# Value products of an attention kernel over 512 queries at a time, on one Trainium2 core

## The chip, the cores and the metric

The kernel runs on one core of one Trainium2 chip. Five engines work side by side and meet at semaphores: TensorE (matrix products; PE in the profile, its weight loads PEld), VectorE (DVE), ScalarE (ACT), GpSimd (POOL) and SyncE (SP), which here issues nearly all DMAs. The metric is the device time of one execution in microseconds; lower is better.

## The reference

One layer of an encoder: RMS norm, multi-head latent attention with a SiLU gate, output projection, residual, final RMS norm. Sequence 1024, width 1024, 8 heads, all float32. What matters here:

```
q  = rms_norm(c_q)  @ w_uq      # per head 128 "nope" + 64 rotary columns
kv = rms_norm(c_kv) @ w_ukv     # per head 128 key + 128 value columns
s  = q_nope @ k_nope.T + q_pe @ k_pe.T
p  = softmax(s * scale)         # 1024 x 1024 per head
o  = p @ v
y  = (o * silu(gate)) @ w_out + x
out = rms_norm(y)
```

## The kernel before

**Precision by splitting.** Each operand of a product is split into a high part, rounded to the matmul's input type, and a low part, the remainder. `mm3` (lines 58 to 61) makes a product from three matmuls: high by high, high by low, low by high. So the probabilities too must be split before they meet the values.

**Stages.** Up to about 193 us the kernel makes the latent projections, the rotary parts and the gate (`stream`, `rope_half`). From then to about 525 us it runs attention, and after that the output projection (`out_start`, `out_end`, `out_last`).

**Attention.** The work is cut into 64 units `u`, eight per head, each of 128 queries by 1024 keys. `scores(u)` makes ten matmuls of 512 columns into a PSUM tile `s`; VectorE takes the row maxima (`nmx`, line 462), ScalarE the exponentials with row sums (line 464), VectorE the reciprocal (line 469), GpSimd multiplies by it (line 470), and VectorE transposes 32 by 32 blocks in place (line 471). The result goes to one of two buffers `probs`.

Four units make a *group* of 512 queries; there are 16 groups. In a 32 by 32 transposed tile the keys lie on partitions inside each 32-row block only, so `exchange(g)` moves blocks between partitions by 16 DMAs of 128 KB on SP's queue, into tiles `d`. Before the change there are two tiles `d` per group, one for each pair of 32-query blocks `a` (index `two`), from a pool of two buffers of 8 KB per partition. So the tile of a half takes the room of the same half of the group before, and its DMAs wait until that half has been split.

`split_part(g, two)` splits one half's `d` into two pairs of tiles `pt_h`, `pt_l`, one for each half of the keys: ScalarE casts (line 489), VectorE subtracts (line 491, and half of the second at line 493), GpSimd subtracts the other half (line 494). There are three buffers of each. `values(g, two)` multiplies: 8 key tiles by 3 matmuls of 256 columns into half a PSUM bank `pv`, then two VectorE multiplications into `gate` (line 512).

**Order.** The loop over `u` issues `scores(u)`; `exchange(u // 4)` at every fourth unit; `split_part` at odd units from 7; `values` at even units from 8. The order on each engine isn't this one: a planner at build time sorts the instructions by priority and by when its own model says that their inputs are ready. `later(100)` puts `values` 100 steps back in priority, `later(150)` the loads of `qpe`. Production of q, k and v for the next heads (`produce_q`, `produce_k`, `produce_v`) and, at the last head, the loads of output weights (`load_w_out`, line 519) and of x (line 542) lie between. Each engine then runs its list strictly in the planned order.

**Memory.** SBUF is nearly full. Two unnamed tiles `pad_a` and `pad_b` only take up room.

Of the kernel before, what the change touches and what calls it, by code (L numbers as in the profile page):

```python
# [8 lines left out]
F32 = mybir.dt.float32  # L9
F32R = mybir.dt.float32r  # L10
# [4 lines left out]
P = 128  # L15
L = 1024
# [7 lines left out]
KD = D // P  # L24
HT = L // 2
# [4 lines left out]
def kernel(  # L30
# [21 lines left out]
    nc = tc.nc  # L52
    mm = nc.tensor.matmul

    def f32(ap):
        return ap.bitcast(F32)

    def mm3(ps, lh, ll, rh, rl, first, last):
        mm(ps, lhsT=lh, rhs=rh, start=first, stop=False)  # L59
        mm(ps, lhsT=lh, rhs=rl, start=False, stop=False)  # L60
        mm(ps, lhsT=ll, rhs=rh, start=False, stop=last)  # L61
# [5 lines left out]
    def later(steps):  # L67


        def wrap(fn):  # L70
            def run(*args):
                tc.cur_priority += steps
                result = fn(*args)
                tc.cur_priority -= steps
                return result

            return run

        return wrap

    const = ctx.enter_context(tc.tile_pool(name="const", bufs=1))
# [5 lines left out]


    g_sb = const.tile([P, KD + 5], F32, name="g_sb")
    const.tile([P, 72], F32, name="pad_a")  # L90
    qpe_d = dram.tile([H, 4, 32, L], F32, name="qpe_d")

    row_d = {name: dram.tile([P, KD], F32, name=f"{name}_d") for name in ("rx", "sq", "sk", "rq", "rk")}
    kk_h = const.tile([P, L], F32R, name="kk_h")
    kk_l = const.tile([P, L], F32R, name="kk_l")
    ss = const.tile([P, 2, KD], F32, name="ss")
    const.tile([P, 112], F32, name="pad_b")

    def acc(name):
        return ps_a.tile([P, 512], F32, name=name, tag="acc")  # L100

    def wide(name):
        return ps_s.tile([P, L], F32, name=name, tag="s")

    def halves(half):
        return slice(half * HT, (half + 1) * HT)
# [87 lines left out]
    gate = gpool.tile([P, H, L], F32, name="gate")  # L194
# [56 lines left out]
    def stream(m):  # L251
        wh, wl = [], []
        for kq in range(2):
            wh.append(gp.tile([P, 4, P], F32R, name=f"gwh_{m}_{kq}", tag="gwh"))
            wl.append(gp.tile([P, 4, P], F32R, name=f"gwl_{m}_{kq}", tag="gwl"))
            wr = gp.tile([P, 4, P], F32, name=f"gwr_{m}_{kq}", tag="gwr", bufs=2)
            nc.sync.dma_start(wr, wg[m - 3 - (m > 5), :, kq * 4:(kq + 1) * 4])
            split(wr, wh[-1], wl[-1])
        ps = wide(f"g_{m}")
        for k in range(KD):  # L260
            for half in range(2):
                hs = halves(half)
                mm3(ps[:, hs], wh[k // 4][:, k % 4], wl[k // 4][:, k % 4], xh[:, k, hs], xl[:, k, hs],
                    k == 0, k == KD - 1)
        return ps
# [8 lines left out]
    ps = stream(3)  # L274
    nc.scalar.copy(craw[3], ps)
    latent_sums((0, 1, 2), "sq")
    ps = stream(4)
# [11 lines left out]
    ps = wide("pe")  # L289
# [74 lines left out]
    for i in range(1, H):  # L364
# [7 lines left out]
        if i < 5:  # L372
            g, half = (i - 1) // 2, (i - 1) % 2
# [11 lines left out]
    at = ctx.enter_context(tc.tile_pool(name="attn", bufs=2, side="right"))  # L385
# [2 lines left out]
        return columns.tile([P, 1], F32, name=name, tag=name)  # L388

    def split_tiles(name):  # L390
        hi = at.tile([P, 2, HT], F32R, name=f"{name}_h", tag="pt_h", bufs=3)
        lo = at.tile([P, 2, HT], F32R, name=f"{name}_l", tag="pt_l", bufs=3)
        return hi, lo

    def produce_v(tiles, two, w):
# [51 lines left out]
    square, part = {}, {}  # L447
# [25 lines left out]
    def exchange(g):  # L473

        src = square.pop(g).rearrange("p j k t c -> p j (k t c)")
        for two in range(2):
            d = part[g, two] = at.tile([P, 2, L], F32, name="d", tag="d")
            for a in range(2):
                for j in range(4):
                    r0 = (two * 2 + a) * 32  # L480
                    nc.sync.dma_start(d[j * 32:(j + 1) * 32, a], src[r0:r0 + 32, j])

    def split_part(g, two):
        d = part[g, two]
        part[g, two] = []
        for kh in range(2):
            src = d[:, :, halves(kh)]
            hi, lo = split_tiles("pt")
            nc.scalar.copy(hi, src)  # L489
            if kh == 0:  # L490
                nc.vector.tensor_sub(lo, src, f32(hi))  # L491
            else:
                nc.vector.tensor_sub(lo[:, 0], src[:, 0], f32(hi[:, 0]))
                nc.gpsimd.tensor_sub(lo[:, 1], src[:, 1], f32(hi[:, 1]))  # L494
            part[g, two].append((hi, lo))

    @later(100)
    def values(g, two, v):
        h = g // 2
        pt = part.pop((g, two))  # L500
        ps = acc("pv")[:, 0:256]
        for kt in range(8):
            c0 = (kt % 2) * 256 + (h % 2) * P
            vh, vl = v[kt // 2]
            hi, lo = pt[kt // 4]
            ks = slice(kt % 4 * P, (kt % 4 + 1) * P)
            mm3(ps.rearrange("p (a q) -> p a q", a=2), vh[:, c0:c0 + P], vl[:, c0:c0 + P],
                hi[:, :, ks], lo[:, :, ks], kt == 0, kt == 7)
        for a in range(2):
            c0 = (g % 2) * 512  # L510
            gs = gate[:, h, c0:c0 + 512].rearrange("p (t a c) -> p t a c", t=4, a=4)[:, :, two * 2 + a]
            nc.vector.tensor_mul(gs, ps[:, a * P:(a + 1) * P].rearrange("p (t c) -> p t c", t=4), gs)

    w_o = [[], []]
    started = []
# [118 lines left out]
    for u in range(U + 10):  # L634
        h, i = u // 8, u % 8
# [12 lines left out]
        if u % 4 == 3 and u < U:  # L648
            exchange(u // 4)
        if u % 2 == 1 and u >= 7:  # L650
            g, two = (u - 7) // 4, (u - 7) % 4 // 2
            if g < U // 4:
                split_part(g, two)
        if u % 2 == 0 and u >= 8:
            g, two = (u - 8) // 4, (u - 8) % 4 // 2
            if g < U // 4:
                values(g, two, v_of[g // 4])
# [107 lines left out]
```

## Time and profile before

| | us |
|---|---|
| runs | 599.02, 598.67, 598.40 |
| median | 598.67 |
| profiled execution | 599.3 |
| its span (first to last instruction) | 597.3 |
| TensorE busy | 579.0 |
| VectorE busy | 433.0 |
| ScalarE busy | 277.3 |
| GpSimd busy | 218.9 |
| mean granted TensorE clock | 0.992 |

A row of a group reads: line, engine, operation, output<-inputs, shapes, count, then busy time, mean nanoseconds of one, and the idle time of the engine just before with what ended it. A row of a timeline begins with the start and the duration in us; in brackets stands the idle time before it and what ended it. A row of waits is: who waited, on whom, total us, times, longest. Matmul durations overlap one another, so their sum is more than the time they take; the distance from start to start tells what one costs in a stream.

### The profile page before, as it was taken

The page shows a single profiled execution, that of the slowest core. Times are in us where ns is not written, and L with a number is a line of the kernel's source. Part 1 is how long each engine was busy: PE and PEld are TensorE (multiplying, and loading weights), DVE is VectorE, ACT ScalarE, POOL GpSimd, SP SyncE. Part 2 cuts the span into 40 slices and gives each one's busy share as a digit, 9 for nine tenths or more (in the row PEclk, how much of TensorE's full clock was granted, in tenths as well). Part 3 has the DMA queues.
Part 4 walks back from the last instruction along what each step waited for, and adds up shares of the span by engine and source line. Part 5 has one row for each costly group of instructions (what it writes and reads, how often), then busy time and mean ns, then how long its engine had stood idle before and what let it go on. Part 6 is the DMA issues. An engine that isn't in the chain of part 4 may idle for free.

```text
span 597.3 us, 8664 instructions
## 1 busy us (share of the span) xinstructions
PE 579.0 (97%) x2988; PEld 494.0 (83%) x2988; DVE 433.0 (72%) x632; ACT 277.3 (46%) x435; POOL 218.9 (37%) x195
## 2 busy tenths in 40 slices
PE   8999999979999998999999999999999989999995
PEld 5888888858888887888988989888888968978885
DVE  5813579926205889899878899898987996783663
ACT  4347553111103464456454545454545673653642
POOL 3414504514101344544334354434442662563000
PEclk9999999979999999999999999999999999999999
DMA  8846322233202166466654747456646975431332
GB/s 300 277 128 233 106 75 68 64 143 109 108 18 71 40 160 146 110 148 153 145 128 107 180 107 160 93 115 166 143 93 138 275 174 141 120 104 53 124 140 105
DMA packets 35534, 78.71 MB, mean 132 GB/s; under 512 B 7266, under 2 KB 10850, under 8 KB 35428
## 3 DMA queue, kind: packets, MB, share of 16 engines
q1 hardware_dynamic: 34196, 76.08, 47.3%
q10 hardware_dynamic: 1296, 2.10, 1.0%
q8 instruction: 23, 0.38, 0.3%
q14 instruction: 19, 0.16, 0.1%
HBM read 36.19 MB, written 8.41 MB: 75 GB/s over the span
## 4 chain that ended last, share of the span: by engine, by line
PE 77%; DVE 8%; DMA 6%; issue 3%; SPq 2%; ACT 2%; POOL 0%; ACTq 0%; DVEq 0%; POOLq 0%
PE s L59 4%; PE s L60 4%; PE s L456 4%; PE pv L59 4%; PE s L457 4%; PE s L61 4%; PE pv L60 4%; PE pv L61 4%; PE o L61 4%; PE o L60 4%; PE g L59 4%; PE g L60 4%; PE o L59 4%; PE g L61 4%; PE q L60 2%
## 5 line engine op out<-in xcount | busy, mean ns | idle before, releaser
L470 POOL TENSOR_SCALAR probs<-probs,rc 128x1024 f32<-128x1024 f32 x64 | 80.9, 1268 | 111.0 <-DVE rc L469 85.3
L464 ACT ACTIVATE probs<-s,nmx 128x1024 f32<-128x1024 f32 x64 | 71.3, 1114 | 72.8 <-DVE nmx L462 69.5
L489 ACT CAST pt_h<-d 128x1024 fp32r<-128x1024 f32 x64 | 66.0, 1051 | 46.3 <-PE pv L61 19.9
L471 DVE STREAM_TRANSPOSE probs<-probs 128x1024 f32<-128x1024 f32 x64 | 78.9, 1233 | 6.5 <-POOL probs L470 5.9
L462 DVE TENSOR_REDUCE nmx<-s 128x1 f32<-128x1024 f32 x64 | 76.9, 1207 | 7.5 <-PE s L457 7.4
L59 PE MATMUL pv<-pt_h,v_h 128*128 128x256 f32 x256 | 72.6, 284 | 2.3 <-ACT pt_h L489 2.3
L60 PE MATMUL pv<-pt_l,v_h 128*128 128x256 f32 x256 | 72.5, 283 | 0.6 <-DVE pt_l L491 0.5
L61 PE MATMUL pv<-pt_h,v_l 128*128 128x256 f32 x256 | 72.4, 283 | 0.0
L494 POOL TENSOR_TENSOR pt_l<-d,pt_h 128x512 fp32r<-128x512 f32 x32 | 46.0, 1438 | 46.1 <-ACT pt_h L489 29.4
L59 PE MATMUL g<-xh,gwh 128*128 128x512 f32 x160 | 62.8, 392 | 0.0
L60 PE MATMUL g<-xl,gwh 128*128 128x512 f32 x160 | 62.7, 392 | 0.0
L61 PE MATMUL g<-xh,gwl 128*128 128x512 f32 x160 | 62.5, 391 | 0.0
L59 PEld LDWEIGHTS pv<-pt_h,v_h 128*128 128x128 f32 x256 | 48.9, 191 | 4.4 <-ACT pt_h L489 3.2
L59 PE MATMUL s<-k_h,q_h 128*128 128x512 f32 x128 | 50.1, 394 | 1.9 <-ACT probs L464 1.9
L60 PEld LDWEIGHTS pv<-pt_l,v_h 128*128 128x128 f32 x256 | 48.9, 191 | 2.9 <-DVE pt_l L491 0.8
L61 PEld LDWEIGHTS pv<-pt_h,v_l 128*128 128x128 f32 x256 | 48.9, 191 | 2.0
L60 PE MATMUL s<-k_l,q_h 128*128 128x512 f32 x128 | 50.3, 393 | 0.0
L456 PE MATMUL s<-kk_h,qpe 128*128 128x512 f32 x128 | 50.2, 392 | 0.0
L457 PE MATMUL s<-kk_l,qpe 128*128 128x512 f32 x128 | 50.1, 391 | 0.0
L61 PE MATMUL s<-k_h,q_l 128*128 128x512 f32 x128 | 49.9, 390 | 0.0
L491 DVE TENSOR_TENSOR pt_l<-d,pt_h 128x1024 fp32r<-128x1024 f32 x32 | 45.1, 1410 | 5.2 <-ACT pt_h L489 4.6
L60 PE MATMUL o<-wol,o_split 128*128 128x512 f32 (+1 forms) x118 | 44.8, 379 | 0.0
(191 smaller groups left out, 1293.0 us busy)
## 6 DMA issues: line engine op xcount, KB each, us to landing
d<-probs SPq DMA_DIRECT2D x256, 128.0 KB
gwr<-in_wg SPq DMA_DIRECT2D x20, 256.0 KB
craw_b<-in_x SPq DMA_DIRECT2D x8, 512.0 KB
qpe<-qpe_d SPq DMA_DIRECT2D x16, 256.0 KB
wor<-in_wo SPq DMA_DIRECT2D x16, 256.0 KB
xr<-in_x SPq DMA_DIRECT2D x16, 256.0 KB
xr<-in_xT SPq DMA_DIRECT2D x7, 512.0 KB
qpe_d<-craw_a SPq DMA_DIRECT2D x8, 256.0 KB
```

The costliest lines, as they stand in the source:

```text
L59: mm(ps, lhsT=lh, rhs=rh, start=first, stop=False)
L60: mm(ps, lhsT=lh, rhs=rl, start=False, stop=False)
L61: mm(ps, lhsT=ll, rhs=rh, start=False, stop=last)
L456: mm(s[:, ks], lhsT=qpe_s, rhs=kk_h[:, ks], start=False, stop=False)
L457: mm(s[:, ks], lhsT=qpe_s, rhs=kk_l[:, ks], start=False, stop=True)
L462: nc.vector.tensor_reduce(nmx, s, axis=AX.X, op=ALU.max, negate=True)
L464: nc.scalar.activation(p_t.rearrange("p j k c -> p k j c"), s.rearrange("p (k j c) -> p k j c", k=8, j=4), AF.Exp, bias=nmx, accum_out=sm,)
L470: nc.gpsimd.tensor_scalar(p_t, p_t, rc, 1.0, op0=ALU.mult, op1=ALU.mult)
L471: nc.vector.transpose(out=p_t, in_=p_t)
L489: nc.scalar.copy(hi, src)
L491: nc.vector.tensor_sub(lo, src, f32(hi))
L494: nc.gpsimd.tensor_sub(lo[:, 1], src[:, 1], f32(hi[:, 1]))
```

## The change

The value products take all 512 queries of a group at once, and the two steps of a group are no longer two pairs of query blocks but two halves of the keys.

- `exchange` issues the same 16 DMAs, into one tile `d` of 16 KB per partition for the whole group; there are two buffers of it, so a group takes the room of the group two before.
- `split_part(g, two)` splits two slices of 256 keys, each over all four query blocks, from half `two` of the keys. The tiles keep their size and number, 4 x 256 in place of 2 x 512. The engines' shares are the same.
- `values(g, two)` multiplies four key tiles by 3 matmuls of 512 columns. The first call starts the sum in a whole PSUM bank and leaves it open; the second goes on with it and ends with one VectorE multiplication of 512 columns into `gate`.
- The padding tiles shrink by 128 words in all, and `ss` moves.

```diff
--- before.py
+++ after.py
@@ -87,14 +87,13 @@
 
 
     g_sb = const.tile([P, KD + 5], F32, name="g_sb")
-    const.tile([P, 72], F32, name="pad_a")
+    ss = const.tile([P, 2, KD], F32, name="ss")
+    const.tile([P, 56], F32, name="pad")
     qpe_d = dram.tile([H, 4, 32, L], F32, name="qpe_d")
 
     row_d = {name: dram.tile([P, KD], F32, name=f"{name}_d") for name in ("rx", "sq", "sk", "rq", "rk")}
     kk_h = const.tile([P, L], F32R, name="kk_h")
     kk_l = const.tile([P, L], F32R, name="kk_l")
-    ss = const.tile([P, 2, KD], F32, name="ss")
-    const.tile([P, 112], F32, name="pad_b")
 
     def acc(name):
         return ps_a.tile([P, 512], F32, name=name, tag="acc")
@@ -388,8 +387,8 @@
         return columns.tile([P, 1], F32, name=name, tag=name)
 
     def split_tiles(name):
-        hi = at.tile([P, 2, HT], F32R, name=f"{name}_h", tag="pt_h", bufs=3)
-        lo = at.tile([P, 2, HT], F32R, name=f"{name}_l", tag="pt_l", bufs=3)
+        hi = at.tile([P, 4, 256], F32R, name=f"{name}_h", tag="pt_h", bufs=3)
+        lo = at.tile([P, 4, 256], F32R, name=f"{name}_l", tag="pt_l", bufs=3)
         return hi, lo
 
     def produce_v(tiles, two, w):
@@ -473,43 +472,45 @@
     def exchange(g):
 
         src = square.pop(g).rearrange("p j k t c -> p j (k t c)")
-        for two in range(2):
-            d = part[g, two] = at.tile([P, 2, L], F32, name="d", tag="d")
-            for a in range(2):
-                for j in range(4):
-                    r0 = (two * 2 + a) * 32
-                    nc.sync.dma_start(d[j * 32:(j + 1) * 32, a], src[r0:r0 + 32, j])
+        d = part[g] = at.tile([P, 4, L], F32, name="d", tag="d")
+        for a in range(4):
+            for j in range(4):
+                nc.sync.dma_start(d[j * 32:(j + 1) * 32, a], src[a * 32:(a + 1) * 32, j])
 
     def split_part(g, two):
-        d = part[g, two]
-        part[g, two] = []
-        for kh in range(2):
-            src = d[:, :, halves(kh)]
+
+        for c in range(2):
+            src = part[g][:, :, (two * 2 + c) * 256:(two * 2 + c + 1) * 256]
             hi, lo = split_tiles("pt")
             nc.scalar.copy(hi, src)
-            if kh == 0:
+            if c == 0:
                 nc.vector.tensor_sub(lo, src, f32(hi))
             else:
-                nc.vector.tensor_sub(lo[:, 0], src[:, 0], f32(hi[:, 0]))
-                nc.gpsimd.tensor_sub(lo[:, 1], src[:, 1], f32(hi[:, 1]))
-            part[g, two].append((hi, lo))
+                nc.vector.tensor_sub(lo[:, 0:2], src[:, 0:2], f32(hi[:, 0:2]))
+                nc.gpsimd.tensor_sub(lo[:, 2:4], src[:, 2:4], f32(hi[:, 2:4]))
+            split_keys.append((hi, lo))
+
+    split_keys, open_pv = [], {}
 
     @later(100)
     def values(g, two, v):
         h = g // 2
-        pt = part.pop((g, two))
-        ps = acc("pv")[:, 0:256]
-        for kt in range(8):
+        ps = acc("pv") if two == 0 else open_pv.pop(g)
+        for kt in range(two * 4, two * 4 + 4):
             c0 = (kt % 2) * 256 + (h % 2) * P
             vh, vl = v[kt // 2]
-            hi, lo = pt[kt // 4]
-            ks = slice(kt % 4 * P, (kt % 4 + 1) * P)
-            mm3(ps.rearrange("p (a q) -> p a q", a=2), vh[:, c0:c0 + P], vl[:, c0:c0 + P],
+            if kt % 2 == 0:
+                hi, lo = split_keys.pop(0)
+            ks = slice(kt % 2 * P, (kt % 2 + 1) * P)
+            mm3(ps.rearrange("p (a q) -> p a q", a=4), vh[:, c0:c0 + P], vl[:, c0:c0 + P],
                 hi[:, :, ks], lo[:, :, ks], kt == 0, kt == 7)
-        for a in range(2):
-            c0 = (g % 2) * 512
-            gs = gate[:, h, c0:c0 + 512].rearrange("p (t a c) -> p t a c", t=4, a=4)[:, :, two * 2 + a]
-            nc.vector.tensor_mul(gs, ps[:, a * P:(a + 1) * P].rearrange("p (t c) -> p t c", t=4), gs)
+        if two == 0:
+            open_pv[g] = ps
+            return
+        del part[g]
+        c0 = (g % 2) * 512
+        gs = gate[:, h, c0:c0 + 512].rearrange("p (t a c) -> p t a c", t=4, a=4)
+        nc.vector.tensor_mul(gs, ps.rearrange("p (a t c) -> p t a c", a=4, t=4), gs)
 
     w_o = [[], []]
     started = []
```

## The prediction

> **What bounds the kernel now.** I read the page's parts 1 and 2, the waits of TensorE, a table of windows for the attention stage (193 to 525 us), and then the order of time on single engines.
>
> ```profile
> PE 579.0 (97%) x2988; PEld 494.0 (83%) x2988; DVE 433.0 (72%) x632; ACT 277.3 (46%) x435; POOL 218.9 (37%) x195
> ```
> ```profile
> PE 77%; DVE 8%; DMA 6%; issue 3%; SPq 2%; ACT 2%; POOL 0%; ACTq 0%; DVEq 0%; POOLq 0%
> ```
> ```profile
> PE pv L59 <- ACT pt_h L489: 2.3, 2, 1.2
> PE s L59 <- ACT probs L464: 1.9, 2, 1.2
> PE pv L60 <- DVE pt_l L491: 0.5, 1, 0.5
> ```
> ```profile
> 300.00:460.00 160.00, 160.00 (x929) 141.53 (x929) 140.50 (x194) 82.20 (x122) 67.43 (x56) 1.00 0.56 128
> ```
>
> The chain that ended last is 77% TensorE. The third fence is all that TensorE waited for between 190 and 530 us: 4.7 us. From 300 to 460 us (columns: length, PE, PEld, DVE, ACT, POOL, clock) TensorE never pauses and VectorE has 88%. So the stage is the sum of TensorE's steps plus these few waits. Durations of matmuls overlap, so their price is the step from start to start:
>
> ```profile
> 312.65 0.28 PE L60 MATMUL pv<-pt_l,v_h 128*128 128x256 f32 x1
> ...
> 313.97 0.28 PE L59 MATMUL pv<-pt_h,v_h 128*128 128x256 f32 x1
> ```
> ```profile
> 307.66 0.40 PE L59 MATMUL s<-k_h,q_h 128*128 128x512 f32 x1
> ...
> 309.73 0.39 PE L457 MATMUL s<-kk_l,qpe 128*128 128x512 f32 x1
> ```
> ```profile
> 149.83 0.39 PE L61 MATMUL g<-xh,gwl 128*128 128x512 f32 x1
> ...
> 152.78 0.39 PE L59 MATMUL g<-xh,gwh 128*128 128x512 f32 x1
> ```
>
> Twelve value products take 11 steps in 1.32 us: 0.120 us each at 256 columns. At 512 columns, ten score products give 9 steps in 2.07 us, 0.230; fourteen gate products, of the stage before, 13 in 2.95, 0.227.
>
> **Part 1, the products.** 768 value products of 256 columns become 384 of 512. A pair cost 0.240 us and the product that replaces it 0.230 (the score products run in the same stage, so I take their step): 384 x 0.010 = **-3.8 us**. Bounds: -5.0 with the gate's 0.227, and 0 if the long step should cost a full pair. TensorE has no cover over this stage, so the saving is on the path. The moving operand is now four runs of 128 columns, not two; the 256-column step with two runs is about half of the unbroken 512-column step, so I price runs at nothing.
>
> The Trainium skill, "TensorE: Matmul & The Clock Gate", section "Back-to-back issue gap", gives columns / 2.4 ns plus about 2.5 ns per warm matmul; by that the saving would be only 384 x 2.5 ns = 1.0 us, an estimate from that page. The rows differ: two halves cost 10 ns more than a whole.
>
> **Part 2, the evacuation.** The 64 multiplications into gate become 16 of 512 columns.
>
> ```profile
> L512 DVE TENSOR_TENSOR gate<-pv,gate 128x128 f32<-128x128 f32 x64 | 15.5, 277 | 1.5 <-PE pv L61 1.5
> ```
> ```profile
> L577 DVE TENSOR_TENSOR y_sb<-o,xr 128x512 f32<-128x512 f32 x8 | 5.4, 682 | 2.9 <-PE o L61 2.9
> ```
>
> Per group 4 x 277 = 1108 ns become about 682 (a PSUM-fed two-input operation of that size): 16 x 0.43 = 6.8 us less on VectorE, which isn't the bound: 0 in the sum. The sum's bank is now held from a group's first half to its second. Four banks of that kind exist and TensorE waited for none in the fence above, so 0. At most this part gains the 0.5 us that TensorE waited for VectorE's pt_l, or costs one more wait of the size seen (1.2).
>
> **Part 3, the splits.** Still 64 ScalarE casts of 1024 elements, 32 VectorE subtractions of 1024, and 32 halves each on VectorE and GpSimd; three buffers each, each used up by 1.4 us of products as before: 0. Bounds: the elements are the same and only runs and order differ, so the longest single wait, 1.2 us, either way.
>
> **Part 4, the exchange.** The same 16 DMAs per group with the same shapes, now into one tile of all four query blocks. Two things follow.
>
> (a) The first split of a group needs sixteen landings instead of eight.
>
> ```profile
> 227.89 10.06 SPq L481 DMA_DIRECT2D d<-probs  x16
> ```
> ```profile
> 235.12 1.99 ACT L489 CAST pt_h<-d 128x1024 fp32r<-128x1024 f32 x2 [3.81 <-issue]
> 237.02 1.11 ACT L464 ACTIVATE probs<-s,nmx 128x1024 f32<-128x1024 f32 x1
> ```
> ```profile
> 236.21 0.39 PE L59 MATMUL pv<-pt_h,v_h 128*128 128x256 f32 x1 [1.17 <-ACT pt_h L489]
> ```
>
> Groups 0 and 1 are the first of sixteen. In group 1 SP issues for 10.06 us, so the eighth DMA leaves at 232.9 and the cast starts at 235.12, 2.2 us later. For the sixteenth that is 238.0 + 2.2 = 240.2: 5.0 us later, at a place where TensorE already waited 1.17 us. What can stand in is what follows there:
>
> ```profile
> L60 PE MATMUL q<-cq_l,wq_h 128*128 128x512 f32 x3 | 1.2, 393 | 0.0
> ...
> L59 PE MATMUL s<-k_h,q_h 128*128 128x512 f32 x2 | 0.8, 390 | 0.0
> ```
>
> From 236.4 to 240.75 us there are three forms of q products with x3 and five of s with x2: 19 products x 0.229 = 4.35 us that need no probabilities of group 1. If they move ahead, 5.0 - 4.35 = 0.7 us is left. Groups 0, 2 and 3 lie in the same thin start of the pipeline; I take 0.7 for three groups, **+2.1 us**. Later groups are covered by their lead:
>
> ```profile
> L489 ACT CAST pt_h<-d 128x1024 fp32r<-128x1024 f32 x64 | 66.0, 1051 | 46.3 <-PE pv L61 19.9 <-DMA d<-probs 11.8 <-issue 5.2
> ```
>
> The casts there wait for buffers that value products free (19.9 us), more than for DMAs (11.8): their data lie ready. If that cover goes, each group pays up to 5.0 us. Bounds of (a): 0, and 5.0 in three groups, 15 us. At the end, group 15's casts come 5 us later too; the 24 o products that stand between 508 and 522 us need none of its queries (5.5 us at 0.230), so 0, at worst 5.0.
>
> (b) The tile of a group takes the room of the group two before, no longer that of half the group just before.
>
> ```profile
> SPq L481 <- DVE pt_l L493: 33.7, 13, 5.4
> ```
> ```profile
> 456.47 4.95 SPq L481 DMA_DIRECT2D d<-probs  x8
> 462.29 1.76 SPq L519 DMA_DIRECT2D wor<-in_wo  x4
> ...
> 466.78 7.03 SPq L481 DMA_DIRECT2D d<-probs  x8
> ```
> ```profile
> 478.22 1.05 ACT L489 CAST pt_h<-d 128x1024 fp32r<-128x1024 f32 x1 [2.72 <-DMA d<-probs]
> ```
> ```profile
> 480.59 0.39 PE L60 MATMUL pv<-pt_l,v_h 128*128 128x256 f32 x1 [0.55 <-DVE pt_l L491]
> 483.45 0.50 PE L59 MATMUL s<-k_h,q_h 128*128 128x512 f32 x1 [1.17 <-ACT probs L464]
> 490.81 0.39 PE L59 MATMUL pv<-pt_h,v_h 128*128 128x256 f32 x1 [1.18 <-ACT pt_h L489]
> ```
>
> SP stood 33.7 us before second halves waiting for the last split; that wait goes. Mostly it hid behind TensorE, but in group 13 the second eight came after loads of output weights and x, the cast waited 2.72 us, an exponential stood behind it, and TensorE lost 0.55 + 1.17 us. With sixteen in one block from 456.5 to 466.6 that goes: **-1.7 us** (bounds 0 and -1.7). What is late next is group 14, where 1.18 us stays. Behind the longer block on SP wait a qpe load and weight loads for the next head; TensorE waits for neither now: 0, at most 1.2.
>
> **Sum.** -3.8 + 2.1 - 1.7 = -3.4 us against the profiled execution's 599.3 (span 597.3): 595.9. The median of the runs is 598.67, 0.6 less, so **595.3 us**.
>
> **Rivals.**
> - *Slower: group 1's cast blocks ScalarE.* ScalarE works in order; the row at 235.12 shows 3.81 us in which the next exponential stood behind the cast. If the order keeps the cast there, TensorE gets neither values nor scores, and idles 1.17 + 5.0 us. What a gap of that kind does, the trace shows once:
>
> ```profile
> 123.33 0.39 PE L61 MATMUL g<-xh,gwl 128*128 128x512 f32 x1
> 128.08 0.79 PE L59 MATMUL ab<-cq_h,wq_h 128*128 128x512 f32 x1 [4.37 <-POOL wq_h L64]
> ...
> 133.79 0.53 PE L60 MATMUL g<-xl,gwh 128*128 128x512 f32 x1
> ```
>
>   After 4.37 us idle, 14 products to 133.79 step by 0.43 us instead of 0.227: 14 x 0.2 = 2.8 us more. The price is 5.0 + 2.8 for group 1 and 1.4 for two others, so -3.8 - 1.7 + 9.2 = +3.7: 602.4 us. It decides against the change once (a) passes 5.5 us. Against it: the order is planned anew for the later landing. The Trainium skill, "TensorE: Matmul & The Clock Gate", section "HAM oscillation", says that idle gaps beyond about 3.4 us drop the clock to half; the trace agrees, with 4.37 us slowing and 1.17 us not.
> - *No change.* A 512-column step that costs what two of 256 cost (0.240) leaves -1.7 + 2.1 = +0.4 us: 599.1. For it: pv's operand is broken and the score's isn't; against it, the 512-column rows above show 0.227 and 0.230. With the page's 2.5 ns it is -0.6 us, so this case holds that rule too.
> - *Faster still.* The new plan hides (a) and every present wait, and a product costs the gate's 0.227: -5.0 - 4.7 = -9.7, 589.0 us. For it: VectorE is relieved by 6.8 us and SP by 33.7.
>
> **How the numbers follow.** Forecast 0.47, slower 0.28, no change 0.13, faster still 0.12. The measurement of this kernel tells 0.2%, 1.2 us, from no change. So faster 0.47 + 0.12 = 0.59, same 0.13, slower 0.28. The forecast's own range is 593 to 597.4 (part 1 at -5.0 with (a) at 1.0 on one side, (a) at 4.2 on the other, each still 0.6 under the profile's own time); to hold 8 in 10 it reaches to 589.5 and 603.0.
>
> **What would show it.** 384 value products stepping by about 0.230 us; 16 multiplications of some 680 ns; no SP wait on the last split; group 13's sixteen issues in one block; TensorE's waits in 190 to 530 us near 5 us, those before 300 us grown and those at 480 us gone. Wrong if the step is 0.240, or if a gap of over 4 us with slow steps behind it appears between 207 and 280 us.

## The result and the profile after: slower, by about 1%

The changed kernel takes 604.08 us (median of four runs, 603.67 to 606.37), the kernel before beside it 598.85 us. The ratio, here and below taken over all the runs and not from the medians, is 1.0096, with a 95% interval of 1.0070 to 1.0122. Predicted were 595.3 us and a range of 589.5 to 603.0. The profiled execution of the changed kernel took 603.67 us, its span is 601.9 us.

Busy times and the chain that ended last, from the page after:

```profile
PE 578.0 (96%) x2604; PEld 475.5 (79%) x2604; DVE 429.5 (71%) x584; ACT 276.2 (46%) x435; POOL 223.7 (37%) x195
...
PE 59%; DVE 12%; SPq 11%; DMA 8%; issue 5%; ACT 4%; POOL 1%; ACTq 0%; POOLq 0%; DVEq 0%
```

TensorE had 77% of the chain before. Now VectorE, the DMA queue and the DMAs have 31% together (16% before): more of the chain runs through the exchange. TensorE's waits between 190 and 530 us, as they were listed for the kernel before:

```profile
PE s L59 <- ACT probs L463: 4.1, 5, 2.0
PE pv L59 <- ACT pt_h L485: 4.1, 4, 2.1
PE o L61 <- DVE o_split L568: 1.7, 1, 1.7
PE o L59 <- ACT probs L463: 1.4, 1, 1.4
```

That is 11.3 us in place of 4.7. But the products themselves became cheaper, the new value products and the old score products alike (timeline of TensorE after):

```profile
307.03 0.39 PE L59 MATMUL s<-k_h,q_h 128*128 128x512 f32 x1
...
309.29 0.39 PE L59 MATMUL s<-k_h,q_h 128*128 128x512 f32 x1
...
311.79 0.39 PE L60 MATMUL pv<-pt_l,v_h 128*128 128x512 f32 x1
...
314.28 0.39 PE L59 MATMUL pv<-pt_h,v_h 128*128 128x512 f32 x1
```

Ten steps of score products take 2.26 us and eleven steps of value products 2.49 us, so 0.226 us each. To see where time went I cut both traces at the start of the last exponential (unit 63). Windows before, then after: length, PE, PEld, DVE, ACT and POOL busy, granted clock, share of the DMA engines and GB/s. The first window starts at the first exponential, the second ends a little after the start of the last product.

```profile
193.80:492.60 298.80, 294.00 (x1687) 258.45 (x1686) 266.09 (x366) 160.91 (x240) 133.34 (x110) 1.00 0.59 139
492.60:590.90 98.30, 98.01 (x497) 83.37 (x496) 63.08 (x129) 48.38 (x107) 27.38 (x25) 1.00 0.37 112
```
```profile
193.00:493.30 300.30, 290.68 (x1345) 240.16 (x1343) 260.58 (x322) 158.44 (x239) 135.62 (x108) 0.99 0.58 138
493.30:595.50 102.20, 100.25 (x454) 83.03 (x454) 63.70 (x124) 49.73 (x108) 29.17 (x26) 0.98 0.36 108
```

From the first exponential to the last, TensorE is busy for 3.3 us less (294.00 to 290.68) and needs 1.5 us longer: its idle time there doubled from 4.8 to 9.6 us. Behind the last exponential 3.9 us are added: 2.2 us more of busy time and 1.65 us more idle. With 0.8 us less ahead of the first exponential the sum is +4.6 us, the difference of the spans.

Not all of the busy time is work. In each of the two windows of the changed kernel one stretch of 3.4 us ran at half the granted clock, in the kernel before none. The second one, with a wait in front of it:

```profile
494.60:498.00 3.40, 3.40 (x9) 2.62 (x9) 2.51 (x3) 0.00 (x0) 2.08 (x2) 0.50 0.89 210
```

The first lies at 358.10 to 361.50. At half the clock each gives away about 1.7 us of products, 3.4 us together. So the saving is there, and the 4.6 us are roughly what idle time and half speed added beyond it. Of the 2.2 us behind the last exponential, some 1.7 us are this; most of the rest is that two output products were done before it, where it had been eight.

The two thickest places of the idle time in windows of 20 us, after:

```profile
340.00:360.00 20.00, 17.87 (x75) 14.29 (x74) 17.70 (x23) 10.22 (x15) 9.42 (x7) 0.95 0.71 161
...
480.00:500.00 20.00, 13.66 (x49) 9.55 (x48) 17.19 (x22) 8.45 (x14) 9.45 (x8) 0.91 0.67 166
```

At 355 us TensorE waits for the first cast of group 7 (timeline of TensorE, then of ScalarE):

```profile
356.99 0.50 PE L59 MATMUL pv<-pt_h,v_h 128*128 128x512 f32 x1 [2.13 <-ACT pt_h L485]
...
358.39 0.63 PE L60 MATMUL q<-cq_l,wq_h 128*128 128x512 f32 x1
...
360.10 0.63 PE L61 MATMUL q<-cq_h,wq_l 128*128 128x512 f32 x1
```
```profile
193.03 1.12 ACT L463 ACTIVATE probs<-s,nmx 128x1024 f32<-128x1024 f32 x1
...
321.81 1.11 ACT L463 ACTIVATE probs<-s,nmx 128x1024 f32<-128x1024 f32 x1 [2.20 <-DVE nmx L461]
...
355.89 2.94 ACT L485 CAST pt_h<-d 128x1024 fp32r<-128x1024 f32 x3 [3.76 <-DMA d<-probs]
...
493.33 1.11 ACT L463 ACTIVATE probs<-s,nmx 128x1024 f32<-128x1024 f32 x1 [1.48 <-DVE nmx L461]
...
498.03 2.95 ACT L485 CAST pt_h<-d 128x1024 fp32r<-128x1024 f32 x3 [3.49 <-DMA d<-probs]
```

From 358.39 to 360.10 four steps take 1.71 us, 0.43 each, half speed. The q products that follow need no probabilities: they stood behind a value product in TensorE's list, and the list runs in order. Group 7's sixteen DMAs were late (after, SyncE's queue), and so was what fed them: the exponential at 321.81 is that of unit 28, the first unit of group 7.

```profile
343.71 10.16 SPq L478 DMA_DIRECT2D d<-probs  x16
```

### The profile page after: what moved, and what is told of

The parts are those of the page before. It is cut to its first block, busy times and chain, and to the rows that moved or that the text cites. A ratio compares the mean times of both kernels' runs of the same rounds, so it can differ in the third digit from the quotient of the medians.

```text
span 601.9 us, 7663 instructions
## 1 busy us (share of the span) xinstructions
PE 578.0 (96%) x2604; PEld 475.5 (79%) x2604; DVE 429.5 (71%) x584; ACT 276.2 (46%) x435; POOL 223.7 (37%) x195
## 3 DMA queue, kind: packets, MB, share of 16 engines
HBM read 36.19 MB, written 8.41 MB: 74 GB/s over the span
## 4 chain that ended last, share of the span: by engine, by line
PE 59%; DVE 12%; SPq 11%; DMA 8%; issue 5%; ACT 4%; POOL 1%; ACTq 0%; POOLq 0%; DVEq 0%
SPq L478 11%; PE o L60 5%; PE o L59 5%; PE o L61 5%; PE g L59 4%; PE g L60 4%; PE g L61 4%; PE pv L59 2%; PE pv L60 2%; DMA d<-probs 2%; PE pv L61 2%; PE s L59 2%; DVE probs L470 2%; PE s L60 2%; PE s L455 2%
## 5 line engine op out<-in xcount | busy, mean ns | idle before, releaser
L485 ACT CAST pt_h<-d 128x1024 fp32r<-128x1024 f32 x64 | 65.5, 1049 | 35.5 <-DMA d<-probs 15.8
L490 POOL TENSOR_TENSOR pt_l<-d,pt_h 128x512 fp32r<-128x512 f32 x32 | 49.7, 1554 | 41.2 <-ACT pt_h L485 34.1
L59 PE MATMUL pv<-pt_h,v_h 128*128 128x512 f32 x128 | 50.4, 394 | 4.1 <-ACT pt_h L485 4.1
L60 PE MATMUL pv<-pt_l,v_h 128*128 128x512 f32 x128 | 50.0, 390 | 0.1
L61 PE MATMUL pv<-pt_h,v_l 128*128 128x512 f32 x128 | 49.9, 390 | 0.0
L487 DVE TENSOR_TENSOR pt_l<-d,pt_h 128x1024 fp32r<-128x1024 f32 x32 | 40.3, 1258 | 9.5 <-ACT pt_h L485 8.5
L59 PE MATMUL o<-woh,o_split 128*128 128x512 f32 (+1 forms) x118 | 45.5, 385 | 1.4 <-ACT probs L463 1.4
L61 PE MATMUL o<-woh,o_split 128*128 128x512 f32 (+1 forms) x118 | 44.9, 384 | 1.7 <-DVE o_split L568 1.7
L568 DVE TENSOR_TENSOR o_split<-gate,o_split 128x512 fp32r<-128x512 f32 (+2 forms) x48 | 30.9, 673 | 7.9 <-ACT o_split L567 7.9
```

The costliest lines, as they stand in the source:

```text
L490: nc.gpsimd.tensor_sub(lo[:, 2:4], src[:, 2:4], f32(hi[:, 2:4]))
```

## The experiments

Each kernel was timed against the kernel before on the same chip. "The exchange" below means one tile `d` per group with sixteen DMAs in a block.

### First question: which part of the change costs

**The exchange alone.** Splits and products as before, by query halves and 256 columns, from the new tile `d`.

```diff
+            hi = at.tile([P, 2, HT], F32R, name="pt_h", tag="pt_h", bufs=3)
...
+        ps = acc("pv")[:, 0:256]
+        for kt in range(8):
...
```

> Keeps the changed kernel's exchange (one tile of the whole group, room of the group two before) and goes back to the old products: 256 columns, by query halves, in all 16 groups. Theory L (what costs is that the first split of a group needs sixteen landings instead of eight): the first split needs eight again and SP is no longer held back, so 596 to 599 us, and TensorE's waits between 190 and 530 us fall back from about 11 us to 5 or less. Rival R (the new room and layout of the tiles, or the order planned from them, cost the time): 603 us or more with the old products too.

Measured: 599.23 us, ratio 0.9997 [0.9985, 1.0009], and TensorE's waits between 190 and 530 us are 4.3 us, as theory L had it. The exchange by itself costs nothing and brings nothing that could be measured. Its splits need eight landings, so this doesn't test the sixteen.

**Everything but the width.** The exchange and the splits of the change, each product of 512 columns as two of 256.

```diff
-            mm3(ps.rearrange("p (a q) -> p a q", a=4), ..., hi[:, :, ks], lo[:, :, ks], ...)
+            for n in range(2):
+                mm3(ps[:, n * 256:(n + 1) * 256]..., hi[:, 2 * n:2 * n + 2, ks], lo[:, 2 * n:2 * n + 2, ks], ...)
```

> The changed kernel's exchange and splits by key tiles, but each product of 512 columns as two of 256 with the same weights. If TensorE's saving is on the path, this costs 384 x 13 ns = 5 us on top of the changed kernel: 608 to 610 us. If the saving only turned into idle time behind the probabilities (rival S: the softmax chain, not TensorE, sets the pace now), 603 to 605 us, with less idle time.

Measured: 600.28 us, 1.0012 [1.0001, 1.0023]. Neither expectation held. The sixteen landings and the key-tile splits cost about 1 us, barely clear of the noise. The other 4 us come with the wide products, although those are the part that saves TensorE time.

**Old form where the changed kernel idles**, at the end and then in eight groups:

```diff
+HALVES = (14, 15)                      # first kernel
+HALVES = (0, 1, 2, 3, 7, 11, 14, 15)   # second kernel
```

> The changed kernel, with the old split and products (256 columns, query halves) in the last two groups only, 14 and 15. Theory L: the extra 5 us of landing hurt where no later group's work is left, so the idle stretch between 482 and 498 us shrinks by about 5 us: 598 to 600 us. Rival R: 603 to 605. Rival W (the splitting of the output weights holds up the last transposes): 603 to 605 as well, since the transposes come no sooner.

Measured: 604.36 us, 1.0072 [1.0048, 1.0096]. Group 14's cast now starts at 494.03 us, and the last exponential, planned behind it, goes to 495.93 (493.33 in the changed kernel): what was won behind it was lost ahead of it.

> The changed kernel with the old split and products (query halves, 256 columns) in the groups before whose values TensorE stood idle (0 to 3, 7, 11, 14, 15), and the new ones in the other eight. Theory L (the first split needs sixteen landings, and by then TensorE has run out of score products, since two probs buffers let the scores run only one group ahead): the idle time falls from about 17 us to 4 to 7, and eight groups keep a saving of 24 x 13 ns each, 2.5 us: 595 to 599 us. Rival P (the idle time is an accident of the planned order, and every new order puts it elsewhere): 601 us or more, with waits in other groups.

Measured: 606.84 us, 1.0124 [1.0101, 1.0147], no better than the changed kernel (1.0096 [1.0070, 1.0122]) and in the range of rival P. The theory of the landings (L) falls as the whole cause: eight landings instead of sixteen at the places with the idle time don't cure it. The order was planned anew here too, so the landings alone were not isolated.

**Later landings.** Four more DMAs of 128 KB between the eighth and the ninth of each group, in the changed kernel and in the one with the exchange alone.

```diff
+            if a == 2:
+                for j in range(4):
+                    nc.sync.dma_start(more_d[g, j], src[0:32, j])
```

> The changed kernel with four more DMAs of 128 KB per group (copies of blocks to memory that nobody reads), issued between the eighth and the ninth of the exchange. The last landing of a group comes some 2.5 us later. Theory L: five or six groups have a wait that is bare already, so 607 to 618 us. Rival P or R: 603 to 606, since SP and the DMA engines have room.

> The same four more DMAs at the same place, in the kernel with the new exchange and the old split and products by query halves in all groups (599.2 us without them). Theory L: the first split needs the first eight only, which come no later, so the loss is 0 to 3 us: 599 to 602. If four more DMAs hurt for another reason (bandwidth, the queue, the buffers of probs that come free later), the loss is the same as in the changed kernel.

Measured: 605.84 us, 1.0102 [1.0086, 1.0118], and 600.32 us, 1.0013 [0.9988, 1.0037]. Two microseconds more per block cost 1 to 2 us by the medians, in neither kernel clear of the noise, and not 2 us at each thin place. That speaks against L again. As the loss is about the same in both kernels, it doesn't tell sixteen landings from eight.

**Two queues for the exchange.**

```diff
+                q = nc.scalar if j % 2 else nc.sync
```

> The changed kernel, with half of the 16 DMAs of every group issued from ScalarE's queue, so that each queue issues for about 5 us instead of 10. Theory L: the sixteenth lands up to 5 us sooner, the waits of TensorE fall from 11 us to 3 or less: 592 to 598 us. Against it stands ScalarE's own time, 128 issues of about 0.6 us (77 us more on an engine that is busy 276 us), and that an issue on ScalarE waits for the transposes with casts and exponentials behind it: if that decides, 604 us or more. Rivals R and W: 602 to 605.

Measured: 691.86 us, 1.1541 [1.1522, 1.1559]. ScalarE's exponentials stood behind its DMAs, 160.6 us in all (one place of ScalarE's timeline):

```profile
336.84 8.41 ACTq L479 DMA_DIRECT2D d<-probs  x8
345.30 1.11 ACT L463 ACTIVATE probs<-s,nmx 128x1024 f32<-128x1024 f32 x1 [12.24 <-DMA d<-probs]
```

It says nothing on the change, for issuing on ScalarE cost ScalarE the time. That was the losing case of the expectation.

**Loads of the output weights later.** The loop of `load_w_out` at `i == 5` instead of `i == 1`.

> The changed kernel, with the loads and splits of the output weights issued four units later (unit 61 instead of 57). Rival W: VectorE and GpSimd do the last groups' normalisation, transposes and splits without the weights between them, group 14's transposes end about 4 us sooner, 598 to 601 us. Theory L: the landing of sixteen stays at the end of the chain, 602 to 605 us; later weights may also leave TensorE without output products, then above 605.

Measured: 604.49 us, 1.0077 [1.0061, 1.0093]. The planner put every instruction of every engine where it was: this is a second timing of the changed kernel, and its question stayed untested.

### Second question: is it the order that comes with the wide products

The partition so far: every kernel with narrow products throughout takes 599 to 600 us, every one with wide products 604 to 607 (the one on two queues aside). What differs besides the width is TensorE's list. I counted how many units are scored ahead of a group's first value product, less the units of the groups before (4g):

| kernel | group 5 | 7 | 9 | 11 | 13 |
|---|---|---|---|---|---|
| before | 10 | 8 | 10 | 9 | 8 |
| narrow products (600.28 us) | 10 | 8 | 10 | 8 | 9 |
| changed | 8 | 10 | 8 | 10 | 8 |

Ten is as far as the two buffers `probs` let it go: they hold eight units, and two more can stand as scores in the two tiles `s`. No run with two buffers has more. The planner put group 5's first four value tiles ahead of the scores of units 28 and 29 in the changed kernel, behind them in the other two; likewise group 9 and units 44 and 45. Theory O: those units belong to groups 7 and 11, so these groups' exchange comes late, and at ten ahead TensorE has no scores left to fill the time. It was tested from both sides.

**The wide kernel with the order turned back at two places** (e12_order).

```diff
+            if u % 4 == 1 and (u - 9) // 4 in (5, 9):
+                with tc.issue_after(scored[u].ins):
+                    values((u - 9) // 4, 0, v_of[(u - 9) // 16])
```

> The changed kernel with nothing altered but TensorE's order at two places: the first four value tiles of groups 5 and 9 stand behind the scores of units 29 and 45 (ten units scored ahead of them instead of eight), as they do in the kernel with the narrow products. That makes groups 7 and 9 to 11 less or equally hard pressed (group 7's first product has nine units scored ahead of it instead of ten). Theory O (the wide products lose because the order planned around them scores four of every sixteen units late, so that groups 7 and 11 find nothing to do on TensorE): the gap of 2.3 us at 354 us, its half-clock products and the 0.5 us at 436 go; with units 28 to 31 and 44 to 47 earlier the end of attention comes earlier too; 598 to 601 us. Rival W (the wide products themselves are late, whatever the order, since twelve products of 0.227 us have to be there in one piece before a score's slot comes free): 603 to 605 us, the gap at 354 only moved.

Measured: 601.29 us, 1.0032 [1.0018, 1.0045], where the change has 1.0096 [1.0070, 1.0122]. Ahead of groups 5, 7, 9 and 11 stand now 10, 9, 10 and 10 units. Timelines of ScalarE and of SyncE's queue, and the window of the old gap:

```profile
194.11 1.12 ACT L465 ACTIVATE probs<-s,nmx 128x1024 f32<-128x1024 f32 x1
...
320.85 1.12 ACT L465 ACTIVATE probs<-s,nmx 128x1024 f32<-128x1024 f32 x1 [3.51 <-DVE nmx L463]
...
351.21 2.95 ACT L487 CAST pt_h<-d 128x1024 fp32r<-128x1024 f32 x3 [2.15 <-DMA d<-probs]
```
```profile
338.06 11.18 SPq L480 DMA_DIRECT2D d<-probs  x16
```
```profile
340.00:360.00 20.00, 20.00 (x97) 16.86 (x97) 17.92 (x22) 11.13 (x17) 8.18 (x7) 1.00 0.55 127
```

That is just above the range of theory O. The gap at 354 us and its slow products are gone; TensorE's waits between 190 and 530 us are 9.8 us where the changed kernel has 11.3, and of the two half-speed stretches the one at the end is left. The kernel with narrow products, in the same order at these places, waits 5.0 us. Wide, then narrow:

```profile
PE s L59 <- ACT probs L465: 4.8, 6, 2.0
PE pv L59 <- ACT pt_h L487: 1.9, 2, 1.1
PE o L61 <- DVE o_split L570: 1.7, 1, 1.7
PE o L59 <- ACT probs L465: 1.4, 1, 1.4
```
```profile
PE s L59 <- ACT probs L463: 2.8, 3, 1.7
PE o L61 <- DVE o_split L569: 1.6, 1, 1.6
PE o L59 <- ACT o_split L568: 0.6, 1, 0.6
```

So with the order alike the 5 us that the wide products save are waited for instead.

**The mirror: the narrow kernel with the changed kernel's order at the same two places** (e13_narrow_order).

```diff
-        if u < U:
+        if u < U and u not in (28, 44):
             scores(u, q_now, k_now, qpe_now)
...
+        if u in (28, 44):
+            with tc.issue_after(last_pv[0].ins):
+                scores(u, q_now, k_now, qpe_now)
```

> The mirror: the kernel with the exchange and the splits of the change but narrow products (600.28 us), with TensorE's order altered at two places to that of the changed kernel: scores of units 28 and 44 stand behind the first four value tiles of groups 5 and 9 (eight units ahead of them instead of ten; ten ahead of groups 7 and 11). Theory O: TensorE goes idle at groups 7 and 11 as in the changed kernel, 602 to 605 us. Rival W: the order does not matter, 599.5 to 601 us.

Measured: 606.17 us, 1.0119 [1.0098, 1.0140], against 1.0012 for the same products in the other order. Ahead of groups 5, 7, 9 and 11 stand 8, 10, 8 and 10 units, and the gap is back where the changed kernel has it. Timelines of TensorE, ScalarE and SyncE's queue:

```profile
352.04 0.50 PE L59 MATMUL s<-k_h,q_h 128*128 128x512 f32 x1 [1.51 <-ACT probs L463]
...
358.05 0.39 PE L59 MATMUL pv<-pt_h,v_h 128*128 128x256 f32 x1 [1.19 <-ACT pt_h L485]
```
```profile
192.53 1.11 ACT L463 ACTIVATE probs<-s,nmx 128x1024 f32<-128x1024 f32 x1
...
323.80 1.12 ACT L463 ACTIVATE probs<-s,nmx 128x1024 f32<-128x1024 f32 x1 [5.32 <-DVE nmx L461]
...
356.95 2.00 ACT L485 CAST pt_h<-d 128x1024 fp32r<-128x1024 f32 x2 [3.84 <-DMA d<-probs]
```
```profile
344.59 10.33 SPq L478 DMA_DIRECT2D d<-probs  x16
```

For the narrow kernel in its own order the same rows are:

```profile
193.39 1.12 ACT L463 ACTIVATE probs<-s,nmx 128x1024 f32<-128x1024 f32 x1
...
318.01 1.12 ACT L463 ACTIVATE probs<-s,nmx 128x1024 f32<-128x1024 f32 x1 [3.78 <-DVE nmx L461]
...
348.42 1.05 ACT L485 CAST pt_h<-d 128x1024 fp32r<-128x1024 f32 x1 [1.73 <-DMA d<-probs]
```
```profile
335.16 11.28 SPq L478 DMA_DIRECT2D d<-probs  x16
```

The starts of these rows from each kernel's own first exponential, in us:

| kernel | exp of unit 28 | group 7's DMAs | its first cast | time |
|---|---|---|---|---|
| narrow | 124.6 | 141.8 | 155.0 | 600.28 |
| wide, order turned back | 126.7 | 144.0 | 157.1 | 601.29 |
| changed | 128.8 | 150.7 | 162.9 | 604.08 |
| narrow, changed kernel's order | 131.3 | 152.1 | 164.4 | 606.17 |

The first cast goes with the order and not with the width, and the time with the cast. The cost of the order is shown from both sides: with either width the intervals of the two orders lie apart. The width by itself is not: it costs 1 us in the narrow kernel's order (600.28 to 601.29) and brings 2 us in the changed kernel's (606.17 to 604.08), with intervals that overlap both times. One reservation: only the two places were forced; the planner then moved neighbours (group 7's nine instead of eight).

**One of the two places**, group 5's: `in (5,)` in the diff of e12_order.

> One of e12_order's two places alone: group 5's first four value tiles behind the scores of unit 29, group 9 as in the changed kernel. Theory O: the gap of 2.3 us at 354 us and its half-clock products go, the 0.5 us at 436 us and the late units 44 to 47 stay: 602 to 603 us, half of what e12_order won or somewhat more. If the two places do not add (the later one sets the end alone): 603.5 to 605 us.

Measured: 601.02 us, 1.0030 [1.0018, 1.0042]. Group 5's place alone has all of the gain, more than theory O gave it; group 9's adds nothing that could be measured.

### Third question: can it be carried further

**Three buffers `probs`, one tile `d`.**

```diff
+            if u // 4 % 3 == 2:
+                probs = at.tile([P, 4, L], F32, name="probs", tag="probs", bufs=1)
...
+        d = part[g] = at.tile([P, 4, L], F32, name="d", tag="d", bufs=1)
```

> The changed kernel with three buffers for the probabilities of a group and one for their exchanged form (instead of two and two): units can be scored twelve ahead of a group's first product. Theory O: the gaps of the middle (214, 272, 354, 436 us), 8 us with their slow clock, go, and what stays is the end (482 to 498 us), 595 to 599 us. Rival W: wide products are late by themselves, a deeper lookahead changes nothing, 603 to 605 us. With one exchanged buffer a group's sixteen transfers wait for the last split of the group before: if that stands ahead, waits on the DMA queue show it.

Measured: 670.95 us, 1.1195 [1.1169, 1.1220]. Twelve units stood ahead, but the DMAs of a group waited for the last split of the group before (waits of SyncE's queue, 190 to 530 us):

```profile
SPq L482 <- DVE pt_l L493: 61.6, 12, 12.7
```

The single tile cost far more than the lookahead could bring, so this is no test of the lookahead; there was no room for two tiles.

**Nine units ahead in every group**, by putting the scores of every unit 4g+9 behind the first four value tiles of group g.

> The changed kernel with the scores of every unit 4g+9 put behind the first four value tiles of group g: nine units ahead of every group's first product, where the changed kernel has between eight and ten. Theory O: no group is at the end of the lookahead and none is scored late; idle time in the middle under 2 us, 596 to 600 us. Rival W: 603 to 606 us. It can also lose: where the landing is later than the ninth unit's scores, TensorE waits for every group, 607 us or more with a wait for a cast at most groups.

Measured: 620.37 us, 1.0342 [1.0307, 1.0376], the losing case of the expectation. A value product now stands ahead of the next unit's scores, at some groups although those had room: by the ends of the exponentials the score tile was free 1.1 us before the product at 261.23 us and 2.5 us before the one at 492.89. TensorE's waits, 190 to 530 us:

```profile
PE pv L59 <- ACT pt_h L485: 15.1, 9, 4.9
```

**Group 13 too** (`in (5, 9, 13)`; e15_order13), **then groups 2, 6 and 10 as well.**

> The kernel of e12_order (wide products, values of groups 5 and 9 behind the scores of units 29 and 45; 601.29 us) with group 13 treated alike: its first four value tiles behind the scores of unit 61, so units 60 and 61 are scored twelve products (2.7 us) earlier. Theory O: what is left over the narrow kernel lies at the end (TensorE's idle time from 480 to 497 us, 7.1 us beside 4.3 in the narrow one) and is the same late scoring, so it loses another 1 to 3 us: 598 to 600.5 us. Rival V (VectorE's own order holds the last four row maxima behind the splits of the weights, whatever TensorE does): 601 to 602 us with the last exponentials where they were, at 491 us.

Measured: 600.40 us, 1.0018 [1.0004, 1.0032]. From first to last exponential it needs 296.6 us, the kernel with two places 297.1. These two are from the profiled executions, which took 598.40 us, the fastest of twelve, and 601.81. The time is at the edge of what O expected, but the last exponential hardly moved, as V said.

> As e15_order13, with groups 2, 6 and 10 treated alike too: every group up to 13 has ten units scored ahead of its first product, the most that two buffers allow. Theory O as it stands (a score late by a group's four value tiles costs, a score early costs nothing): 597.5 to 600.5 us. Its weak point: at ten ahead TensorE has no score left to take while a landing is late, so that groups 3, 7 and 11 could wait: 600.5 to 603 us with waits of a microsecond or more before the first products of those groups. Rival V: 601 to 603 us.

Measured: 605.35 us, 1.0102 [1.0076, 1.0128], worse than its own worst case. Ten ahead everywhere exhausts the lookahead already at group 2. ScalarE and TensorE there:

```profile
254.27 2.94 ACT L487 CAST pt_h<-d 128x1024 fp32r<-128x1024 f32 x3 [2.57 <-DMA d<-probs]
```
```profile
258.37 0.80 PE L59 MATMUL s<-k_h,q_h 128*128 128x512 f32 x1 [3.29 <-ACT probs L465]
```

A cast that waits for its landing holds up the exponential behind it (at 257.12 us), that holds the score tile, and TensorE idles 3.29 us. So "early scores cost nothing" is wrong as well: with eight ahead at groups 5 and 9, with nine everywhere and with ten everywhere the wide kernel is slower than with the mixture of e15_order13. What makes an order good was not found beyond that.

**Old form at the end, on top of the three places of e15_order13.** `HALVES = (15,)` and `HALVES = (14, 15)`.

> e15_order13 (600.40 us; wide products with three groups' order altered) with the splits and products of group 15 alone in the form of the kernel before: query halves, 256 columns, so that its first products need eight landings, not sixteen. If what is left over the kernel before is the wait for the last landings (TensorE's idle time behind the last exponential was 2.1 us before, 4.5 us in the changed kernel, 3.2 us in e15_order13), this takes a part of it: 598.5 to 600 us. Rival: the output products stand ahead of group 15's values anyway and cover its landings, 600 to 601 us.

> As e18_half15 with group 14 in the old form too. Same theory: 597.5 to 599.5 us, so at or a little below the kernel before (599.3 us). Rival, from e2_halves_end: group 14's casts come sooner and stand ahead of the last exponential on ScalarE, so that it comes later by what is won behind it: 600 to 602 us.

Measured: 601.06 us, 1.0038 [1.0025, 1.0051], and 600.56 us, 1.0024 [1.0011, 1.0036]: no gain over 600.40, so the times are those of the rivals. In the second kernel the last exponential comes at 493.88 us, in e15_order13 at 489.13, as its rival had it. The idle times that the first expectation names are not those of the windows used here: from the last exponential to the last product TensorE is idle for 0.3 us before, 1.95 us in the changed kernel and 2.5 us in e15_order13. No version of the wide kernel beats the kernel before.

## Why the prediction was wrong

- *Part 1, the step.* Right, and better than put: 0.226 to 0.227 us, the bound I had taken from the gate's products. Score products fell from 0.230 to 0.226 too, which was not foreseen. The estimate by the Trainium skill, "TensorE: Matmul & The Clock Gate", section "Back-to-back issue gap", was 1.0 us saved (the page gives that formula for a product by itself); the rows give 384 x (0.240 - 0.227) = 5.0 us of TensorE time.
- *Part 1, "TensorE has no cover over this stage, so the saving is on the path".* This is the step that failed. A busy share of 100% from 300 to 460 us says that TensorE had work to take, not that less work ends the stage sooner. Even with the order turned back, the saved 5 us came back as idle time: TensorE's waits are 9.8 us beside 5.0 with narrow products, and the kernel takes 601.29 us beside 600.28, where the sum had -3.8. Most of these waits are for `probs` and `pt_h`, so the next limit is taken to be the loop through exponential, transposition, sixteen DMAs and cast, which has two `probs` buffers of slack. That is argued from the waits; the one run with more buffers changed `d` too and doesn't show it.
- *What the sum left out: the new order.* I held the planned order fixed except around group 1. It was planned anew with the change, and two places of it were worth 3 us with wide products and 6 us with narrow ones. With wide products the 3 us are 1.5 us of waits (11.3 against 9.8) and one half-speed stretch, about 1.7 us. In the forecast of -3.4 us this term stood at nothing; measured were +5.2. Taken in this order, the exchange and the splits cost 1 us, the wide products 1 us, and the new order 3 us.
- *Part 2.* Right (groups after), and worth nothing, as put:

```profile
L513 DVE TENSOR_TENSOR gate<-pv,gate 128x512 f32<-128x512 f32 x16 | 10.7, 666 | 0.1
```

- *Part 3, 0.* Right: casts of 1049 ns (1051 before) and subtractions of 1258 ns on VectorE (1410) and 1554 ns on GpSimd (1438), and no wait of TensorE for `pt_l` any more.
- *Part 4(a), +2.1 us for sixteen landings.* About 1 us by the narrow kernel against the exchange alone (1.0012 against 0.9997, intervals that just overlap). But the place was wrong: TensorE's waits before 300 us grew from 1.9 us to 2.6 only, and in the narrow kernel the larger ones lie behind 480 us.
- *Part 4(b), -1.7 us.* The cue came out as forecast: no wait for the last split is left on SyncE's queue, and group 13's sixteen go out in one block (SyncE's queue after):

```profile
456.09 10.05 SPq L478 DMA_DIRECT2D d<-probs  x16
...
485.44 10.41 SPq L478 DMA_DIRECT2D d<-probs  x16
```

  The gain did not come: group 14's block now starts at 485.44 (482.13 before), its first cast waits 3.49 us before 498.03, and TensorE's idle time between 480 and 500 us is 6.3 us. With the exchange alone the ratio was 0.9997.
- *The rival "slower".* Its sign was right, and so was its mechanism in part: a cast that waits for its landing on ScalarE, then half speed. Its place was not (355 and 480 to 498 us, not 207 to 280 us): in group 1, of which it spoke, TensorE doesn't wait any more (none from 220 to 260 us). That its 602.4 us come near the 604.08 is therefore luck. The order "planned anew for the later landing", which I held against it, was itself a cost.
- *The end, "0, at worst 5.0".* Behind the last exponential 3.9 us were lost, of which 1.65 us is idle time. The old form in the last groups did not win them back, so the landings are not shown to be the cause. Some 1.7 us of the 3.9 are the half-speed stretch at 494.60, behind waits of 1.36 and 1.72 us.

Left open: why the planner puts group 5's values first when the products are wide (its model of the durations was not looked into), and what a deeper lookahead would give if there were room for it.

## What to carry to other kernels

An engine that is busy all the time in a stage may bound it only until something is taken away; look for the next loop and for its slack in buffers before a saving is counted. When a build-time planner orders the work, a change in one duration can change the whole order: compare the lists, count what stands ahead of each dependent block, and force the old order at the differing places, in both kernels, to tell the order from the operation. A place at which an engine's list puts a waiting instruction ahead of ready ones can cost more than the change saves.

## What was not expected of the hardware

- How long TensorE stood idle did not by itself decide whether it slowed. In the changed kernel an idle time of 2.13 us was followed by half speed (steps of 0.43 us from 358.39 to 360.10), in e15_order13 one of 1.77 us (eight such steps from 472.60). In the kernel with four more DMAs and old products one of 3.44 us, before 488.68, was not: the products behind it step by 0.23 us and the granted clock stays at 1.00. The mirror kernel's waits of 1.51 and 1.19 us left it at 1.00 too. The windows of these two, more DMAs first:

```profile
480.00:500.00 20.00, 16.56 (x95) 14.33 (x94) 20.00 (x27) 9.78 (x14) 12.66 (x8) 1.00 0.84 201
```
```profile
340.00:360.00 20.00, 17.30 (x87) 14.14 (x86) 17.80 (x22) 7.79 (x13) 8.66 (x8) 1.00 0.64 144
```

  My prediction quoted the Trainium skill ("TensorE: Matmul & The Clock Gate", section "HAM oscillation") with gaps beyond about 3.4 us, and found the trace in agreement, with 4.37 us slowing and 1.17 not. The rows of 2.13 and 1.77 us disagree, and the one of 3.44 us, which lies at that figure, didn't slow it. What decides was not looked into.

- Sixteen DMAs of 128 KB were issued hardly faster from two queues at once than from one: eight on each took 8.06 us (SyncE) and 8.41 us (ScalarE, the row above), sixteen on SyncE's queue alone 10.16 us in the changed kernel.
